# Two scans and an attention: products of the inverses further apart, chain operations ahead on VectorE, weighted values in runs of four

## The chip, the core and the metric

The kernel runs on one core of a Trainium2 chip. The metric is the time of one execution on the device in microseconds (us): the median of several runs of the kernel, and beside it one profiled execution, from which the trace is. TensorE is called PE, its weight loads PEld, VectorE DVE, ScalarE ACT, GpSimd POOL; SP issues the DMAs.

## The reference, cut to what matters

Two blocks follow each other on 2048 tokens of width 1024, all in fp32. The first holds two scans over 256 context tokens and the 2048, in both directions, with 4 heads of width 128 each. The gated delta rule (called gdn below) solves a triangular system in every chunk and then carries a state from chunk to chunk; the gated linear attention (gla) carries one too:

```
A  = strict lower part of (k beta) k^T * decay               # per chunk and head
w, u = (A + I)^-1 [k beta exp(G), v beta]                    # the inverse
v_new = u - w S ;  o = (q exp(G)) S + attn v_new             # the chain over the chunks
S  = S exp(g_last) + k_decayed^T v_new
```

The second block's part of interest is a causal attention of 8 heads, queries and keys of width 96, values of width 64:

```
sc = q k^T / sqrt(96), masked where key > query
o  = softmax(sc) v
out_a = o * silu(z_a)
```

## The kernel before, in words

Matrices that are worth it are split into a high and a low part in the type fp32r, and a product is three matmuls (mm3, lines 188 to 190). The program is written through a layer that schedules: each engine but PE in certain stages gets its order from a planned run of the whole program, in which an instruction with a higher priority goes first among those that are ready. Under manual_schedule PE takes its instructions in the order in which the code emits them. On the chip every engine then works strictly in that order.

**The scans** (lines 885 to 1280, 1055 to 2153 us) are emitted by weave: a planner with a clock of its own. Three streams run: gdn_inverse, gdn_scan and gla_scan. Each is a generator that emits some products and yields (cost, lateness, condition); it may go on when cost and LATE (900 ns) times the lateness have passed on the planner's clock. Between them the planner emits a filler, the projections of rest(): triples of 512 columns (tile d), which are also interleaved where the streams' work is ahead of a share of 0.91. The kernel's chunks are of 128 tokens, 18 for each head and direction.

gdn_inverse makes the inverses of two chunks at a time, 72 times. From the inverses of the 32-wide diagonal blocks (X, Pm = its transpose, E = the part above them) it takes a Neumann series: the product lv1 gives Yt (copied by ACT), then R = X - Yt^T R (direction 0, line 964) or R = 1 - ... (direction 1, lines 975 and 981), each R a tensor_sub on DVE that reads the product lv and is the input of the next. It may be two chunks ahead of gdn_scan. gdn_scan has per chunk the products pa (then r on DVE, line 1022), pv (vn on ACT), pS (the new state S on DVE, line 1037) and po. gla_scan works per block of 256 tokens; its factors (function factors: x, l2, the running sum E, I, F, kc, qs, qh, qc, qk) are made a block ahead on DVE, ACT and POOL, and its products are px, pt, go.

**The attention** (3216 to 3800 us) goes through 8 heads h and 4 groups g of 512 queries. One unit is one block of 128 keys (kb): scores makes the three products into st, ACT takes the exponential into pT, and POOL or DVE adds it up into acc. weigh multiplies pT with the values, in fp32, into one half of po's partitions: even and odd blocks go to different halves of 64 columns of PE, so two neighbours can run side by side. Maxima, queries and keys of later groups (tiles sx, ms) are emitted ahead of the scores, spread evenly over time. weigh is emitted for two blocks at a time, PVL = 4 units after the second. gather comes GL = 2 units later: it adds the halves of po into o2, transposes acc, sums it, takes the reciprocal l4 and spreads it over 64 columns into li; finish, FL = 3 units later for a pair of heads, turns li by a product with the identity and scales o2 with it. po has one buffer, pT six.

Of the kernel before, what the change touches and what calls it, by code (L numbers as in the profile page):

```python
# [21 lines left out]
P = 128  # L22
# [23 lines left out]
SXB = 3  # L46
STB = 2
POB = 1
PTB = 6
QB = 5  # L50
PVL = 4
GL = 2
LIP = 0
AD = 3
VB = 2
DPB = 3
# [6 lines left out]
SHARE = 0.91  # L63
BEG = 37000.0
VBF = 2
PRB = 2
GLEAD = 0
WPRI = 1000
# [24 lines left out]
def block_kernel(ctx: ExitStack, tc: tile.TileContext, A, out):  # L93
# [791 lines left out]
    with ExitStack() as gctx:  # L885
        BW = 256
        nch = BW // P
        with tc.tile_pool(name="c1", bufs=2, side="right") as c1, tc.tile_pool(name="c1s", bufs=1, space=PSUM) as c1s, \
# [25 lines left out]
            def gdn_inverse():  # L914


                B4 = [P, 2, 4, 32]

                def load(t):
                    d, h, i, n = step_at(t)  # L920
                    gdn_blocks(t)
                    gdn_blocks(t + 2)
                    m = n - n % 2
                    Xc, Pc = (x[:, m % 4:m % 4 + 2, :].unsqueeze(2).to_broadcast(B4) for x in blocks[h, d, n // 4])
                    N = c1.tile([P, 2, P], F32, tag="N", name="N", bufs=1)
# [12 lines left out]
                def times(lv, a, b):  # L938
                    for c in range(2):
                        pe.matmul(out=lv[:, c], lhsT=a[:, c], rhs=b[:, c], start=True, stop=True)  # L940

                def sums(tag="lv2"):
                    return c1s.tile([P, 2, P], F32, tag="lv", name=tag)

                one = ident.unsqueeze(1).to_broadcast([P, 2, P])
                nxt = load(0)
                for t in range(0, STEPS, 2):
                    d, h, i, n = step_at(t)
                    X, Pm, E = nxt
                    yield 0.0, 0.0, lambda: t <= at[0] + AHEAD  # L950


                    Yt = new("Yt", 1)
                    if d == 0:
                        lv = sums("lv1")
                        times(lv, E, Pm)
                        act.copy(out=Yt, in_=lv)
                        yield 427.0, 1.0
                        R = X
                        for j in range(3):  # L960
                            lv = sums()
                            times(lv, Yt, R)
                            R = new("R") if j < 2 else new("I")
                            dve.tensor_sub(R, X, lv)
                            if j < 2:
                                yield 427.0, 1.0
                        I = R
                    else:

                        lv = c1s.tile([P, 4, P], F32, tag="lv", name="lv1")  # L970
                        times(lv[:, 2:4], Pm, E)
                        times(lv[:, 0:2], E, Pm)
                        act.copy(out=Yt, in_=lv[:, 2:4])
                        R = new("R")
                        dve.tensor_sub(R, one, lv[:, 0:2])  # L975
                        yield 853.0, 1.0
                        for j in range(2):
                            lv = sums()
                            times(lv, Yt, R)
                            R = new("R")  # L980
                            dve.tensor_sub(R, one, lv)
                            yield 427.0, 1.0
                        lv = sums("lv3")
                        times(lv, X, R)
                        I = new("I")
                        act.copy(out=I, in_=lv)
                    inv[t], inv[t + 1] = I[:, n % 2], I[:, 1 - n % 2]
                    if t + 2 < STEPS:
                        nxt = load(t + 2)
                    yield 427.0, 1.0  # L990

            def gdn_scan():
                def load(t):
# [18 lines left out]
                for t in range(STEPS):  # L1012
# [6 lines left out]
                    if i:  # L1019
                        pa = c1s.tile([P, P], F32, tag="pa", name="pa")  # L1020
                        pe.matmul(out=pa, lhsT=kT, rhs=S, start=True, stop=True)
                        dve.scalar_tensor_tensor(out=r, in0=pa, scalar=c_r[:, d, h, n:n + 1], in1=r, op0=ALU.mult,
                                                 op1=ALU.add)
                        yield 213.0, 1.0
                    pv = c1s.tile([P, P], F32, tag="pa", name="pv")
                    pe.matmul(out=pv, lhsT=X, rhs=r, start=True, stop=True)
# [3 lines left out]
                    if i < NCH - 1:  # L1030
# [3 lines left out]
                        if i == 0:  # L1034
                            dve.tensor_copy(out=Sn, in_=ps)
                        else:
                            dve.scalar_tensor_tensor(out=Sn, in0=S, scalar=eGt[:, d, h, n:n + 1], in1=ps, op0=ALU.mult,
                                                     op1=ALU.add)
                    if n < NT:
                        po = c1s.tile([P, P], F32, tag="po", name="po")  # L1040
                        pe.matmul(out=po, lhsT=pr[:, 1, :], rhs=S, start=True, stop=False)
# [639 lines left out]
    with ExitStack() as actx:  # L1681
# [116 lines left out]
                              in0=ps[0:4, 0:P].unsqueeze(1).to_broadcast([4, 4, P]),  # L1798
                              in1=dmask.unsqueeze(2).to_broadcast([4, 4, P]), op=ALU.mult)

        LI = (dve, pool)[LIP]
        acc_, po_, pT_, o_ = {}, {}, {}, {}

        def scores(h, g, kb):
# [43 lines left out]
        def gather(h, g):  # L1848
# [2 lines left out]
            m, r0_ = h // 2, (h % 2) * 64  # L1851
            if r0_ == 0:
                o_[m, g] = (tb.tile([P, GQ], F32, tag=f"o2{g}", name="o2", bufs=1),
                            tb.tile([P, 4, P], F32, tag=f"li{g}", name="li", bufs=1))
            o2, li = o_[m, g]
            rs_, ro = slice(r0_, r0_ + 64), slice(64 - r0_, P - r0_)
            c0 = P if g == 0 else 0
# [9 lines left out]
            for j in range(4):  # L1867
                pe.transpose(out=ps[:, j, :], in_=acc[:, j * P:(j + 1) * P], identity=ident)
            l4 = tb.tile([P, 4], F32, tag="l4", name="l4")
            dve.tensor_reduce(out=l4, in_=ps, op=ALU.add, axis=AX.X)  # L1870
            dve.reciprocal(out=l4, in_=l4)
            LI.tensor_tensor(out=li[:, :, rs_], in0=on64.unsqueeze(1).to_broadcast([P, 4, 64]),
                              in1=l4.unsqueeze(2).to_broadcast([P, 4, 64]), op=ALU.mult)

        def finish(m, g):

            o2, li = o_.pop((m, g))
            gs = slice(g * GQ, (g + 1) * GQ)
            ps = psa.tile([P, GQ], F32, tag="ms", name="ms", bufs=MSB)
            for j in range(4):  # L1880
                pe.matmul(out=ps[:, j * P:(j + 1) * P], lhsT=li[:, j], rhs=ident, start=True, stop=True)
            z = tb.tile([P, GQ], F32, tag="z", name="z")
            sp.dma_start(out=z, in_=d_za[m, :, gs])
            dve.tensor_mul(o2, ps, o2)
# [86 lines left out]
        with tc.manual_schedule(engines=PE_ONLY):  # L1971
# [8 lines left out]
            f0 = ctx.enter_context(tc.tile_pool(name="f0", bufs=2))  # L1980
            tb = actx.enter_context(tc.tile_pool(name="tb", bufs=2))
            psb = actx.enter_context(tc.tile_pool(name="psb", bufs=2, space=PSUM))
            on64 = tb.tile([P, 64], F32, name="on64", tag="on64", bufs=1)
            pool.memset(on64, 1.0)
            for i in range(4):
                value(0, i)
            now, wait, late = 0.0, [], [2, 3, 4, 5, 6]
            for u, (n, h, g, kb) in enumerate(units):
# [10 lines left out]
                scores(h, g, kb)  # L1999
                if h == 0 and g < NG4 - 1 and kb < 4:  # L2000
                    value(0, 4 * g + 4 + kb)
                if kb % 2:
                    wait += [(u + PVL, weigh, (h, g, k)) for k in (kb - 1, kb)]
                    if h == 3 and g == NG4 - 1:
                        wait += [(u + PVL, value, (1, k)) for k in (kb - 1, kb)]
                if kb == 4 * g + 3:
                    wait.append((u + PVL + GL, gather, (h, g)))
                    if h % 2:
# [59 lines left out]
```

## Time and profile before

| | us |
|---|---|
| median of three runs | 3994.24 (3989.38 to 3999.57) |
| profiled execution | 3978.06 |
| its span | 3976.3 |
| PE busy | 3577.2 (90%) |
| DVE busy | 2481.2 (62%) |
| ACT busy | 1373.1 (35%) |
| POOL busy | 1395.6 (35%) |

The span is the time from the first to the last instruction. Busy times are sums over the whole span, which holds stages of different kinds: projections and preparations up to 1055 us, the scans, the merge to about 2670, the second block's projections to 3216, the attention, and the output projection from 3800 on. Matmuls are pipelined: one of 512 columns is shown with some 0.40 us, while the next begins 0.23 us after it; so the distance of two starts tells what an instruction takes away from others, and idle time of PE is counted only from the modelled end. A row of waits names who waited, for whom, the sum in us, how often, and the longest. A product of two fp32 operands has two records, one in fp32r has one.

### The profile page before, as it was taken

To read this page: it belongs to the slowest core of one execution; us is meant where nothing else is said; L and a number is where in the kernel's file an instruction comes from. 1 tells how busy PE (TensorE), PEld (TensorE's weight loads), DVE (VectorE), ACT (ScalarE), POOL (GpSimd) and SP (SyncE) were. 2 spreads that over 40 slices of the span, in tenths; PEclk is the share of its full clock that TensorE was granted. 3 is DMA by queue.
4 is the path that set the end of the run, shared out by engine and by line. 5 is a ranking of instruction groups with operands and counts; after the bars stand their busy time and mean duration, and the time that the engine had idled before them with its cause. 6 is when DMAs were issued, how large, how long until landed. Compare 5 with 4: busy or idle time off the path is not lost.

```text
span 3976.3 us, 57274 instructions
## 1 busy us (share of the span) xinstructions
PE 3577.2 (90%) x18998; PEld 2868.6 (72%) x18998; DVE 2481.2 (62%) x6394; ACT 1373.1 (35%) x3379; POOL 1395.6 (35%) x1666
## 2 busy tenths in 40 slices
PE   4799998888899999988889787878999999999999
PEld 0578877776788887877777677777888765565577
DVE  3645657887776776666665755546405377777766
ACT  0444542221254444444443322212212244444400
POOL 2310124440355555555552311110122246666610
PEclk7899999999999999999999898988999999999999
DMA  5322347763344444544545433324333510001254
GB/s 155 112 61 76 89 139 244 231 183 67 104 135 127 133 130 132 149 136 140 159 142 145 139 103 98 100 88 125 116 103 112 181 47 26 26 18 44 68 170 148
DMA packets 528220, 467.25 MB, mean 118 GB/s; under 512 B 91705, under 2 KB 446371, under 8 KB 527732
## 3 DMA queue, kind: packets, MB, share of 16 engines
q1 hardware_dynamic: 527700, 463.54, 39.3%
q8 instruction: 151, 2.47, 0.3%
q14 instruction: 145, 1.19, 0.1%
q0 software_dynamic: 224, 0.05, 0.0%
HBM read 302.08 MB, written 161.37 MB: 117 GB/s over the span
## 4 chain that ended last, share of the span: by engine, by line
PE 38%; DMA 9%; DVE 8%; issue 4%; ACT 2%; POOL 1%; SPq 0%; DVEq 0%; ACTq 0%; POOLq 0%
PE d L188 4%; PE d L189 4%; PE d L190 4%; PE po L1845 3%; PE acc L188 2%; PE acc L189 2%; PE acc L190 2%; DMA d_h<-xt 2%; PE sx L1782 2%; DMA mg<-d_gate 2%; PE st L1812 2%; PE lv L940 2%; PE st L1813 1%; PE st L1814 1%; DMA o<-d_ob 1%
## 5 line engine op out<-in xcount | busy, mean ns | idle before, releaser
L188 PE MATMUL d<-uBh,whi 128*128 128x512 f32 x832 | 364.2, 438 | 18.3 <-ACT gy L835 13.1
L188 PE MATMUL d<-uAh,whi 128*128 128x512 f32 x832 | 357.9, 430 | 11.6 <-DVE gy L848 6.0
L189 PE MATMUL d<-uAl,whi 128*128 128x512 f32 x832 | 333.9, 401 | 5.8 <-DVE uAl L464 5.8
L189 PE MATMUL d<-uBl,whi 128*128 128x512 f32 x832 | 334.9, 403 | 0.0
L235 POOL TENSOR_TENSOR wlo<-wraw,whi 128x512 fp32r<-128x512 f32 x128 | 168.4, 1316 | 467.9 <-ACT whi L234 442.4
L190 PE MATMUL d<-uAh,wlo 128*128 128x512 f32 x832 | 332.3, 399 | 0.0
L190 PE MATMUL d<-uBh,wlo 128*128 128x512 f32 x832 | 332.3, 399 | 0.0
L1818 ACT ACTIVATE pT<-st 128x512 f32<-128x512 f32 (+1 forms) x320 | 170.0, 532 | 232.2 <-PE st L1814 139.7
L1836 POOL TENSOR_TENSOR acc<-acc,pT 128x512 f32<-128x512 f32 (+1 forms) x168 | 185.9, 1107 | 120.7 <-ACT pT L1818 110.9
L1787 DVE TENSOR_REDUCE mx<-sx 128x1 f32<-128x512 f32 (+3 forms) x288 | 169.4, 616 | 47.5 <-PE sx L1782 29.0
L1388 POOL TENSOR_TENSOR ml<-mg,mh 128x256 fp32r<-128x256 f32 x64 | 57.4, 896 | 395.5 <-ACT mh L1387 305.5
L188 PEld LDWEIGHTS d<-uBh,whi 128*128 128x128 f32 x832 | 161.0, 194 | 43.7 <-ACT gy L835 14.0
L188 PEld LDWEIGHTS d<-uAh,whi 128*128 128x128 f32 x832 | 160.6, 193 | 35.9 <-ACT pre L769 5.1
L190 PEld LDWEIGHTS d<-uBh,wlo 128*128 128x128 f32 x832 | 159.3, 192 | 35.4
L190 PEld LDWEIGHTS d<-uAh,wlo 128*128 128x128 f32 x832 | 159.4, 192 | 33.8
L189 PEld LDWEIGHTS d<-uAl,whi 128*128 128x128 f32 x832 | 160.4, 193 | 26.8 <-DVE uAl L464 6.4
L189 PEld LDWEIGHTS d<-uBl,whi 128*128 128x128 f32 x832 | 161.3, 194 | 20.1 <-DVE uBl L464 0.4
L940 PE MATMUL lv<-R,Yt 128*128 128x128 f32 x576 | 100.2, 298 | 82.1 <-DVE R L975 48.7
L631 DVE SCALAR_TENSOR_TENSOR y<-st,VT,y 128x512 f32<-128x512 f32 (+1 forms) x224 | 165.0, 769 | 4.6
L188 PE MATMUL pp<-yh,w_a_out_h 128*128 128x256 f32 x256 | 84.4, 330 | 91.1 <-DVE mg L1384 89.9
L1845 PE MATMUL po<-pT,v 128*64 128x512 f32 (+3 forms) x640 | 161.0, 562 | 3.3 <-DVE o L1859 3.3
L940 PEld LDWEIGHTS lv<-R,Yt 128*128 128x128 f32 x576 | 81.3, 197 | 110.5 <-DVE R L975 58.2
(593 smaller groups left out, 10620.3 us busy)
## 6 DMA issues: line engine op xcount, KB each, us to landing
wraw<-in_w_in_dram SPq DMA_DIRECT2D x126, 256.0 KB
k<-d_k SPq DMA_DIRECT2D x144, 192.0 KB
d_p<-pre SPq DMA_DIRECT2D x64, 384.0 KB
d_gate<-gy SPq DMA_DIRECT2D x96, 256.0 KB
rows<-d_rows SPq DMA_DIRECT2D x36, 512.0 KB
pr<-d_p SPq DMA_DIRECT2D x128, 128.0 KB
mg<-d_gate SPq DMA_DIRECT2D x64, 256.0 KB
wm<-in_w_mod_dram SPq DMA_DIRECT2D x24, 512.0 KB
```

The source lines that it names most:

```text
L188: pe.matmul(out=out, lhsT=lh, rhs=rh, start=start, stop=False)
L189: pe.matmul(out=out, lhsT=lh, rhs=rl, start=False, stop=False)
L190: pe.matmul(out=out, lhsT=ll, rhs=rh, start=False, stop=stop)
L235: pool.tensor_tensor(out=lo[:, ks, :n], in0=raw[:, :, :n], in1=hi[:, ks, :n].bitcast(F32), op=ALU.subtract)
L631: dve.scalar_tensor_tensor(out=y[:, :w], in0=st[:, o + j:o + j + w], scalar=tap, in1=y[:, :w], op0=ALU.mult, op1=ALU.add)
L940: pe.matmul(out=lv[:, c], lhsT=a[:, c], rhs=b[:, c], start=True, stop=True)
L1782: pe.matmul(out=ps[:, :w], lhsT=qh[0:96, j * P:(j + 1) * P], rhs=kTh[h % 2][0:96, b * 512:b * 512 + w], start=True, stop=not last)
L1787: dve.tensor_reduce(out=m4[:, j:j + 1] if one else mx[:, j, b:b + 1], in_=ps[:, :w], op=ALU.max, axis=AX.X)
L1812: pe.matmul(out=ps[:, c0:], lhsT=kt_h[0:100, ks], rhs=qh[0:100, c0:], start=True, stop=False)
L1818: act.activation(out=pT[:, c0:], in_=ps[:, c0:], func=AF.Exp, scale=SCALE)
L1836: (dve if on_dve else pool).tensor_tensor(out=acc[:, c0:], in0=src[:, c0:], in1=pT[:, c0:], op=ALU.add)
L1845: pe.matmul(out=po_[h, g][r:r + 64, c0:], lhsT=val[kb][:, vs], rhs=pT_.pop((h, g, kb))[:, c0:], start=kb < 2, stop=kb >= 4 * g + 2, skip_g ...
```

## The change

Five edits, in two stages.

1. SLACK = 1.7: gdn_inverse yields this lateness instead of 1.0 after each of its products.
2. The tensor_sub of R in both directions, r and S of gdn_scan are emitted with high priority (PRI = 1000).
3. weigh is emitted for four key blocks at a time, PVL = 3 units after the fourth; pT has 8 buffers. The values of the second four heads, which replace those of the first, follow in fours as well.
4. gather writes the reciprocal straight into li, now two columns a row, one for each head of a pair; the product with ones is gone.
5. finish spreads both columns over 64 each with one copy (lw) on DVE, ahead of its products. The tile of ones and its memset are gone.

```
+SLACK = 1.7
-PTB = 6
+PTB = 8
-PVL = 4
+PVL = 3
...
                         times(lv, E, Pm)
                         act.copy(out=Yt, in_=lv)
-                        yield 427.0, 1.0
+                        yield 427.0, SLACK
                         R = X
                         for j in range(3):
                             lv = sums()
                             times(lv, Yt, R)
                             R = new("R") if j < 2 else new("I")
-                            dve.tensor_sub(R, X, lv)
+                            with tc.high_priority(PRI):
+                                dve.tensor_sub(R, X, lv)
                             if j < 2:
-                                yield 427.0, 1.0
+                                yield 427.0, SLACK
...
-                        dve.tensor_sub(R, one, lv[:, 0:2])
-                        yield 853.0, 1.0
+                        with tc.high_priority(PRI):
+                            dve.tensor_sub(R, one, lv[:, 0:2])
+                        yield 853.0, SLACK
...
-                        dve.scalar_tensor_tensor(out=r, in0=pa, scalar=c_r[:, d, h, n:n + 1], in1=r, op0=ALU.mult,
-                                                 op1=ALU.add)
+                        with tc.high_priority(PRI):
+                            dve.scalar_tensor_tensor(out=r, in0=pa, scalar=c_r[:, d, h, n:n + 1], in1=r, op0=ALU.mult,
+                                                     op1=ALU.add)
...
-            dve.reciprocal(out=l4, in_=l4)
-            LI.tensor_tensor(out=li[:, :, rs_], in0=on64.unsqueeze(1).to_broadcast([P, 4, 64]),
-                              in1=l4.unsqueeze(2).to_broadcast([P, 4, 64]), op=ALU.mult)
+            dve.reciprocal(out=li[:, :, h % 2], in_=l4)
...
+            lw = tb.tile([P, 4, 2, 64], F32, tag="lw", name="lw", bufs=1)
+            dve.tensor_copy(out=lw, in_=li.unsqueeze(3).to_broadcast([P, 4, 2, 64]))
...
-                if kb % 2:
-                    wait += [(u + PVL, weigh, (h, g, k)) for k in (kb - 1, kb)]
+                if kb % 4 == 3:
+                    wait += [(u + PVL, weigh, (h, g, k)) for k in range(kb - 3, kb + 1)]
```

How the order of PE changes in the scans, at the place that the trace has at 1711 us: what stands between the first product of an inverse (lv1) and the next (lv2) in direction 1. Before:

```order
L940 MATMUL lv1_17427<-Pm_17315,E_17316 128x128 x2
L188 MATMUL d_17378<-uBh_758,whi_16993 128x512
L189 MATMUL d_17378<-uBl_759,whi_16993 128x512
L190 MATMUL d_17378<-uBh_758,wlo_16994 128x512
L1231 MATMUL go_17438<-S_17324,qc_17163 128x128
L1232 MATMUL go_17438<-v_17057,at_15581 128x128
L940 MATMUL lv2_17445<-R_17433,Yt_17426 128x128 x2
```

The same on PE of the changed kernel, from the two products go on; ahead of them stand the same lv1 and the same triple (lines from 959 on have moved down by up to five):

```order
L1236 MATMUL go_17438<-S_17322,qc_17174 128x128
L1237 MATMUL go_17438<-v_17057,at_15593 128x128
L1030 MATMUL pv_17451<-r_17384,I_17345 128x128
L188 MATMUL d_17378<-uBh_758,whi_16993 128x512
L189 MATMUL d_17378<-uBl_759,whi_16993 128x512
L190 MATMUL d_17378<-uBh_758,wlo_16994 128x512
L940 MATMUL lv2_17458<-R_17433,Yt_17426 128x128 x2
```

A second triple and pv have come between; they stood behind lv2 before.

On DVE at the second inverse of direction 1, where R (line 975, then 977) is the subtraction and F, qk, x, l2 and qc are factors of gla_scan. Before:

```order
L1125 TENSOR_TENSOR F_15774<-I_15775,E_15731 128x2x4
L1126 TENSOR_TENSOR F_15774<-I_15775 128x2x4
L1131 COPY F_15774<-I_15775 128x2
L1127 TENSOR_TENSOR F_15774<-F_15774 128x2x2
L1129 TENSOR_TENSOR F_15774<-F_15774 128x2x2
L1165 TENSOR_TENSOR qk_15827<-qs_15825,F_15774 128x2x64
L1166 TENSOR_TENSOR qk_15827<-ke_15815,F_15774 128x2x64
L1105 SCALAR_TENSOR_TENSOR x_15969<-x_15969,l1_15978 128x256
L1163 TENSOR_TENSOR qc_15826<-qs_15825,F_15774 128x256
L1106 TENSOR_TENSOR l2_15979<-l2_15979,l1_15978 128x256
L975 TENSOR_TENSOR R_15549<-ident_117,lv1_15543 128x256
```

On DVE of the changed kernel the same subtraction and what follows it:

```order
L1167 TENSOR_TENSOR qs_15825<-qs_15825,q_15821 128x256
L1166 TENSOR_TENSOR qh_15823<-qh_15823,q_15821 128x256
L977 TENSOR_TENSOR R_15546<-ident_117,lv1_15540 128x256
L1230 SCALAR_TENSOR_TENSOR S_15552<-S_15453,F_15227,px_15511 128x128
L1130 TENSOR_TENSOR F_15788<-I_15789,E_15754 128x2x4
L1131 TENSOR_TENSOR F_15788<-I_15789 128x2x4
L1136 COPY F_15788<-I_15789 128x2
L1132 TENSOR_TENSOR F_15788<-F_15788 128x2x2
L1134 TENSOR_TENSOR F_15788<-F_15788 128x2x2
L1170 TENSOR_TENSOR qk_15827<-qs_15825,F_15788 128x2x64
```

R has moved ahead of the chain of F and all that follows from it.

On PE in the attention, around one pair of blocks before (st are scores, po weighted values, ms queries):

```order
L1812 MATMUL st_33754<-qh_33071,kTh0_31605 128x512
L1813 MATMUL st_33754<-ql_33072,kTh0_31605 128x512
L1814 MATMUL st_33754<-qh_33071,kTl0_31607 128x512
L1845 MATMUL po_33728<-pT_33659,v_31971 64x512
L1845 MATMUL po_33728<-pT_33691,v_31977 64x512
L188 MATMUL ms_33765<-ch_31468,wuh_33401 128x512
```

And on PE of the changed kernel, around the run that holds the same two blocks (sx are maxima):

```order
L1818 MATMUL st_33732<-qh_33067,kTl0_31607 128x512
L1849 MATMUL po_33739<-pT_33631,v_31957 64x512
L1849 MATMUL po_33739<-pT_33643,v_31963 64x512
L1849 MATMUL po_33739<-pT_33654,v_31969 64x512
L1849 MATMUL po_33739<-pT_33690,v_31975 64x512
L1787 MATMUL sx_33744<-kTh1_31606,qh_33427 128x384
```

Two runs of two have become one of four, and four blocks of scores now follow each other without weighted values between them.

## Rows read from the trace of the kernel before

**Rows 1.** busy us by engine, PE clock, DMA; scans, then attention

```profile
1055.00:2153.00 1098.00, 985.20 (x6288) 859.94 (x6287) 746.23 (x2169) 505.09 (x1609) 576.87 (x845) 0.98 0.48 137
3216.00:3800.00 584.00, 568.26 (x2750) 342.12 (x2750) 418.32 (x741) 267.57 (x510) 356.02 (x311) 0.98 0.11 36
```

**Rows 2.** who waited for whom in the scans: us in total, times, longest

```profile
PE lv L940 <- DVE R L975: 48.7, 30, 6.3
PE lv L940 <- DVE R L964: 21.5, 27, 2.4
PE lv L940 <- DVE R L981: 11.3, 11, 3.6
PE pS L1032 <- ACT vn L1028: 10.8, 15, 2.1
```

**Rows 3.** groups by line in the scans: busy us, mean ns, idle before

```profile
L940 PE MATMUL lv<-R,Yt 128*128 128x128 f32 x576 | 100.2, 298 | 82.1 <-DVE R L975 48.7 <-DVE R L964 21.5 <-DVE R L981 10.9
L1193 PE MATMUL px<-ident,kc 128*128 128x128 f32 x144 | 40.0, 278 | 0.6 <-DVE S L1225 0.6
L981 DVE TENSOR_TENSOR R<-ident,lv 128x256 f32<-128x256 f32 x72 | 29.9, 416 | 14.6 <-PE lv L940 14.2
```

**Rows 4.** PE in order of time at 1711 us: start, us, line

```profile
1711.47 0.40 PE L190 MATMUL d<-uBh,wlo 128*128 128x512 f32 x1
1711.70 0.38 PE L1231 MATMUL go<-S,qc 128*128 128x128 f32 x2
1711.92 0.39 PE L1232 MATMUL go<-v,at 128*128 128x128 f32 x2
1716.48 0.84 PE L940 MATMUL lv<-R,Yt 128*128 128x128 f32 x4 [4.17 <-DVE R L975]
```

**Rows 5.** instructions of DVE in order of time, the same place

```profile
1712.80 1.03 DVE L1165 TENSOR_TENSOR qk<-qs,F 128x128 f32<-128x128 f32 x1 [2.13 <-ACT F L1132]
1715.68 0.41 DVE L1163 TENSOR_TENSOR qc<-qs,F 128x256 f32<-128x256 f32 x1
1716.02 0.41 DVE L975 TENSOR_TENSOR R<-ident,lv 128x256 f32<-128x256 f32 x1
```

**Rows 6.** instructions of PE in order of time, a pair of weighted values

```profile
3562.62 0.40 PE L1814 MATMUL st<-qh,kTl 96*128 96x512 f32 x1
3562.95 1.08 PE L1845 MATMUL po<-pT,v 128*64 128x512 f32 x4
3563.96 0.27 PE L1796 MATMUL ms<-ident,m 128*4 128x128 f32 x1
```

**Rows 7.** the same, pairs whose later blocks are narrower

```profile
3507.22 1.07 PE L1845 MATMUL po<-pT,v 128*64 128x512 f32 x4
3508.22 0.39 PE L188 MATMUL ms<-wkvh,kvh 128*128 128x256 f32 x1
3510.58 0.65 PE L1845 MATMUL po<-pT,v 128*64 128x256 f32 x4
3511.15 0.38 PE L188 MATMUL ms<-wkvh,kvh 128*128 128x256 f32 x1
```

**Rows 8.** the same, three pairs that stand together at the end

```profile
3787.11 2.36 PE L1845 MATMUL po<-pT,v 128*64 128x512 f32 x12
3789.40 0.51 PE L188 MATMUL acc<-wz,a 128*128 128x512 f32 x1
```

**Rows 9.** weight loads of the weighted values: ns min/median/max, starts

```profile
L1845 PEld LDWEIGHTS po<-pT,v x640: 132/136/232, 3226.2 to 3788.9; 128*64 128x64 f32 x160
```

**Rows 10.** who waited for whom in the attention: us in total, times, longest

```profile
PE po L1845 <- DVE o L1859: 3.3, 3, 2.1
PE sx L1782 <- DVE mx L1787: 4.3, 3, 2.5
PEld st L1812 <- ACT pT L1818: 29.1, 39, 0.8
```

**Rows 11.** a group by line of DVE in the attention

```profile
L1872 DVE TENSOR_TENSOR li<-on,l 128x256 f32<-128x256 f32 x32 | 25.7, 804 | 0.1
```

More of the change, by code (lines that the diff above doesn't have):

```diff
@@ L48 @@
 POB = 1
-PTB = 6
+PTB = 8
 QB = 5
-PVL = 4
+PVL = 3
 GL = 2
-LIP = 0
 AD = 3
@@ L980, in gdn_inverse @@
                             R = new("R")
-                            dve.tensor_sub(R, one, lv)
-                            yield 427.0, 1.0
+                            with tc.high_priority(PRI):
+                                dve.tensor_sub(R, one, lv)
+                            yield 427.0, SLACK
                         lv = sums("lv3")
@@ L989, in gdn_inverse @@
                         nxt = load(t + 2)
-                    yield 427.0, 1.0
+                    yield 427.0, SLACK
             def gdn_scan():
@@ L1021, in gdn_scan @@
                         pe.matmul(out=pa, lhsT=kT, rhs=S, start=True, stop=True)
-                        dve.scalar_tensor_tensor(out=r, in0=pa, scalar=c_r[:, d, h, n:n + 1], in1=r, op0=ALU.mult,
-                                                 op1=ALU.add)
+                        with tc.high_priority(PRI):
+                            dve.scalar_tensor_tensor(out=r, in0=pa, scalar=c_r[:, d, h, n:n + 1], in1=r, op0=ALU.mult,
+                                                     op1=ALU.add)
                         yield 213.0, 1.0
@@ L1036, in gdn_scan @@
                         else:
-                            dve.scalar_tensor_tensor(out=Sn, in0=S, scalar=eGt[:, d, h, n:n + 1], in1=ps, op0=ALU.mult,
-                                                     op1=ALU.add)
+                            with tc.high_priority(PRI):
+                                dve.scalar_tensor_tensor(out=Sn, in0=S, scalar=eGt[:, d, h, n:n + 1], in1=ps,
+                                                         op0=ALU.mult, op1=ALU.add)
                     if n < NT:
@@ L1799, in shift @@
                               in1=dmask.unsqueeze(2).to_broadcast([4, 4, P]), op=ALU.mult)
-        LI = (dve, pool)[LIP]
         acc_, po_, pT_, o_ = {}, {}, {}, {}
@@ L1853, in gather @@
                 o_[m, g] = (tb.tile([P, GQ], F32, tag=f"o2{g}", name="o2", bufs=1),
-                            tb.tile([P, 4, P], F32, tag=f"li{g}", name="li", bufs=1))
+                            tb.tile([P, 4, 2], F32, tag=f"li{g}", name="li", bufs=1))
             o2, li = o_[m, g]
@@ L1879, in finish @@
             ps = psa.tile([P, GQ], F32, tag="ms", name="ms", bufs=MSB)
+            lw = tb.tile([P, 4, 2, 64], F32, tag="lw", name="lw", bufs=1)
+            dve.tensor_copy(out=lw, in_=li.unsqueeze(3).to_broadcast([P, 4, 2, 64]))
             for j in range(4):
-                pe.matmul(out=ps[:, j * P:(j + 1) * P], lhsT=li[:, j], rhs=ident, start=True, stop=True)
+                pe.matmul(out=ps[:, j * P:(j + 1) * P], lhsT=lw[:, j].rearrange("p a b -> p (a b)"), rhs=ident, start=True, stop=True)
             z = tb.tile([P, GQ], F32, tag="z", name="z")
@@ L1982, in block_kernel @@
             psb = actx.enter_context(tc.tile_pool(name="psb", bufs=2, space=PSUM))
-            on64 = tb.tile([P, 64], F32, name="on64", tag="on64", bufs=1)
-            pool.memset(on64, 1.0)
             for i in range(4):
@@ L2001, in block_kernel @@
                     value(0, 4 * g + 4 + kb)
-                if kb % 2:
-                    wait += [(u + PVL, weigh, (h, g, k)) for k in (kb - 1, kb)]
+                if kb % 4 == 3:
+                    wait += [(u + PVL, weigh, (h, g, k)) for k in range(kb - 3, kb + 1)]
                     if h == 3 and g == NG4 - 1:
-                        wait += [(u + PVL, value, (1, k)) for k in (kb - 1, kb)]
+                        wait += [(u + PVL, value, (1, k)) for k in range(kb - 3, kb + 1)]
                 if kb == 4 * g + 3:
```

## The prediction

> **What bounds the kernel now.** I read the busy times of TensorE (PE) first, by stretches, because 90% over the whole span is a mean over stages with different limits. The order of the instructions changes in two stretches alone: the scans (1055 to 2153 us) and the attention (3216 to 3800 us). In the scans PE is busy 985.2 of 1098 us, so 113 us are open; in the attention 568.3 of 584 us, so 16 us are open; VectorE (DVE) is busy 68% and 72% there [rows 1]. The clock was 0.98 in both, the upper level, and the change takes no pause of PE that would tell otherwise. Next I read who waited for whom in the scans. PE stood 48.7 + 21.5 + 11.3 = 81.5 us, in 68 waits, before a product of the inverses (tile lv) until VectorE had written R from the product before it [rows 2]; the group's own row says the same, 82.1 us [rows 3]. That is seven tenths of what PE leaves open there. The third view is the place of one such wait in order of time. The product stands behind five others, a fill of three at 0.23 us each and two small ones at 0.22, and then PE is idle 4.17 us [rows 4]. VectorE in that time first waits 2.13 us for ScalarE, then works through the factors of the other scan, and takes R up only at 1716.02, for 0.41 us [rows 5]. The wait is for VectorE's queue, not for the subtraction. In the attention PE hardly waits; what can be had there is in how its work is packed.
>
> **Scans: the spacing.** The planner emits the next product of an inverse not 0.9 but 1.53 us of planned time after the last (LATE x SLACK). Total work and the rest of PE's order stay: from the end of the inverses on, the same instructions stand at the same rows of the order. At the place above, what stands between two products grows from one fill and two small products, 0.69 + 0.44 = 1.13 us, to two fills and three small ones, 0.69 x 2 + 0.66 = 2.04 us. I counted so through all 216 products that wait for a result of the one before, with 0.23 us for a product of 512 columns, 0.22 for a small one and 0.11 for a transpose [rows 4]: on average 1.42 us before, 2.25 after, at the least 1.02 and 1.82. By kind, the cover grows 1.0 us for L964 and 0.98 for L981 (1.32 to 2.32 for the kind that both feed), and 0.64 for L975 (1.38 to 2.01). A wait shrinks by that, and not below zero. L964: a mean wait of 21.5/27 = 0.80 us is nearly all covered; with a longest of 2.4 I leave 4. L981: 11.3/11 = 1.03; I leave 4. L975: 48.7/30 = 1.62; were all of them longer than 0.64, 30 x 0.64 = 19 would go; I leave 29. Gone: 81.5 - 37 = 44 us. Idle time in the trace begins only at the modelled end of the product before, so short stalls that the pipeline hides are not in the 81.5; that and the next edit bring the term to 50. Bounds: from the side of no gain 0, if what is late is VectorE and comes later by as much; on the other side all 82 + 11 (vn, [rows 2]) = 93.
>
> What the later products make late: the last product of an inverse to the first use of its result had 9.8 (direction 0) and 11.6 us (direction 1) of PE work between them, and now 6.1 and 7.6, by the same count; a result needs about 1 us behind its product. From an inverse's end to the next one's first product there were 5.9 and 6.5 us, now 3.3 and 4.1; the inputs Pm and E stand ready long before, only X waits for the inverse's end, and X is first read one product later. I count both at nothing; if that cover were gone, it would cost 72 inverses x 1 us.
>
> **Scans: the priority.** R, r and S stand ahead of factor work on VectorE wherever both are ready in the planned time. This adds no instruction. At the second inverse of direction 1, R moves ahead of the whole chain of F; at 1716 us it stays behind qk, x and qc as before, so it doesn't cure the longest waits (that is why I leave 29 us to L975). I give it 3 us of the 50 above; bounds -10 to +15, as factors come later by R's 0.42 us [rows 3] each.
>
> **Attention: four key blocks at a time.** A pair of blocks is two products into the two halves of PE's columns, side by side. The pair begins 0.33 us after the product before it, where 0.23 is the rule, and the next product follows 1.01 us after its start [rows 6]: 1.11 us a pair, in time taken from other products. Narrower pairs take 1.00 and 0.57 us [rows 7]. At the kernel's end three pairs of these widths already stand together: 2.29 us [rows 8], against 1.01 + 1.00 + 0.57 and two more beginnings at 0.10, 2.78. So each merge saves 0.49/2 = 0.245 us. The order has 158 runs of them before and 80 after, 78 merges x 0.245 = 19 us. The rule that speaks against it: the Trainium skill, "TensorE: Matmul & The Clock Gate", Part 3, What overlaps and what doesn't, says that a weight load overlaps with a running matmul only where the row groups differ, and all these weights take the same 128 rows. By that rule a junction would show at least one load of 136 ns [rows 9], 78 x 0.136 = 11 us less, and the attention would bring 8 instead of 19; the run of three at the end holds two junctions, and its 2.29 us don't show the loads. Hence 19 stands.
>
> With it go two waits. The first run of a group of queries stood at the same step as the gather that empties po; now it comes two steps behind: 3.3 us [rows 10] go. And in a row of four score blocks without weighted values VectorE's maxima and ScalarE's exponentials get less time: they cost PE 4.3 us for sx, and 29.1 us on the weight loads, which mostly run beside matmuls [rows 10]. I add 4 us; bounds 0 and 20, that is 0.25 us for each of 80 runs, where the merge would be eaten up. pT has 8 buffers and 7 are alive when a run begins.
>
> The broadcast product li (32 x 0.80 = 25.7 us of VectorE [rows 11]) becomes 16 copies of twice its width. In the order the copy stands right behind the reciprocal, three blocks ahead of PE's use, and VectorE has 28% open, so I count it at 0; its cover gone, it would cost 16 x 1 us at most.
>
> **Sum.** 50 + 19 + 3 - 4 = 68 us. The profiled execution took 3978.06 us, 3976.3 of it in the span, so 3910; the median of the runs shown, 3994.24, is 0.41% above it, and on that scale the sum is 3926 us.
>
> **The rivals.** Scan gains given back: VectorE is the engine that is late at [rows 5], and PE's waits turn into later factors. For it: VectorE's 746 us would have to fit in some 1050, 71%, and it works in bursts. Against it: 350 us of VectorE are idle in the scans. Only the attention's 18 would stay: 3960, on the median's scale 3976. More than forecast: the waits for R go altogether, and those for vn with them, 93 + 18 = 111 us: 3883 after scaling; for it the least cover of 1.82 us, against it the 4.17 us. Slower: R, S and r, placed ahead, wait at the head of VectorE's queue for their products, as R does already for 14.2 us [rows 3], and the factors behind them come too late for the transposes of kc (L1193), which wait 0.6 us now [rows 3]. There are 72 blocks of factors; from 1 us a block it eats the whole gain, at 1.5 us it costs 108 against 68: 4034 us. Against it: VectorE's idle time, and factors are made a block ahead.
>
> **How the numbers follow.** Forecast 0.62; gains of the scans given back 0.17; more than forecast 0.13; slower 0.05; a small rest, 0.03, where both parts come to nothing. What a measurement of this kernel can tell from no change is about 0.3%, 12 us. Faster: 0.62 + 0.13 + 12 parts of the 0.17 (18 us is just over the bound) = 0.87; same 0.08; slower 0.05. The range: 3880, all waits gone, to 3986, the attention alone with half of its gain eaten by its own new waits.
>
> **What would show it.** Right: PE's waits on R near 35 us, the scans' stretch near 1050 us, PE still busy 985 in it; 80 runs of x8 at about 1.9 us or less, the attention near 566 us. Wrong: a new large wait before px or pv, R's wait for lv on VectorE far above 25 us in total, or PE idle before sx and st by more than 10 us.

## The result and the profile after

| | median of the runs, us | profiled execution, us |
|---|---|---|
| before | 3996.01 (3989.38 to 3999.57, 4 runs) | 3978.06 |
| after | 3945.17 (3941.75 to 3950.95, 4 runs) | 3950.95 |

The ratio is 0.9876 (95% interval 0.9858 to 0.9894): 49.5 us faster (42 to 57), where 68 were forecast; 3945 lies in the range, 19 us above the predicted time. The profiled execution of before was 18 us under its median and that of after 6 above, so these two traces differ by 27 us only. Sizes are therefore taken from medians and from further traces of both orders; the two traces tell where the time stands.

Busy times by stretch after, answering to [rows 1] (PE, PEld, DVE, ACT, POOL, then PE's granted clock, DMA share, GB/s):

```profile
1054.00:2130.00 1076.00, 985.61 (x6291) 865.37 (x6290) 733.56 (x2168) 503.46 (x1609) 574.93 (x845) 0.97 0.49 139
3196.00:3775.00 579.00, 553.88 (x2762) 360.92 (x2761) 417.17 (x727) 265.67 (x509) 360.96 (x311) 0.97 0.11 37
```

For the same work the scans took 22 us less with PE busy for the same 985 us; the attention took 5 less with PE busy for 14 less. So the scans lost idle time, and the attention lost work but gained idle time. Who waited for whom in the scans after, answering to [rows 2] (total us, times, longest us):

```profile
PE lv L940 <- DVE R L977: 30.1, 21, 4.2
PE pv L1030 <- DVE r L1026: 25.3, 28, 3.6
PE pa L1024 <- DVE S L1042: 5.3, 5, 1.4
PE px L1198 <- DVE S L1228: 4.7, 4, 1.7
PE lv L940 <- DVE R L965: 2.1, 4, 1.0
```

And the group rows of the products that waited, answering to [rows 3] (busy us, mean ns, idle us before); the last one is pv in the kernel before:

```profile
L940 PE MATMUL lv<-R,Yt 128*128 128x128 f32 x576 | 94.1, 287 | 33.6 <-DVE R L977 30.1 <-DVE R L965 2.1 <-DVE R L984 1.0
L1030 PE MATMUL pv<-r,I 128*128 128x128 f32 x288 | 61.4, 296 | 26.3 <-DVE r L1026 25.3 <-DVE I L965 0.5
L1026 PE MATMUL pv<-r,I 128*128 128x128 f32 x288 | 58.7, 286 | 5.5 <-DVE r L1022 4.9 <-DVE I L964 0.5
```

The inverses' wait fell from 82.1 to 33.6 us: 48.5 went, where 44 were forecast. The wait of pv is new in its size: 5.5 us before and 26.3 now, for r of the chain. S is waited for 10.0 us (before 0.6). Some 30 of the 48.5 us that left R are back on r and S.

The longest waits that are left are of the kind at [rows 4, 5]. PE after, in order of time at 1701 us (start, duration, line; in brackets the idle time before; some rows):

```profile
1701.78 0.39 PE L190 MATMUL d<-uBh,wlo 128*128 128x512 f32 x1
1706.39 1.22 PE L940 MATMUL lv<-R,Yt 128*128 128x128 f32 x4 [4.22 <-DVE R L977]
1708.48 0.63 PE L189 MATMUL d<-uBl,whi 128*128 128x512 f32 x1
1708.91 0.63 PE L190 MATMUL d<-uBh,wlo 128*128 128x512 f32 x1
```

DVE in the same time:

```profile
1702.62 1.03 DVE L1170 TENSOR_TENSOR qk<-qs,F 128x128 f32<-128x128 f32 x1 [2.33 <-ACT F L1137]
1703.57 0.81 DVE L1171 TENSOR_TENSOR qk<-ke,F 128x128 f32<-128x128 f32 x1
1704.31 0.94 DVE L1110 SCALAR_TENSOR_TENSOR x<-x,l 128x256 f32<-128x256 f32 x1
1705.17 0.41 DVE L1111 TENSOR_TENSOR l<-l,l 128x256 f32<-128x256 f32 x1
1705.50 0.50 DVE L1168 TENSOR_TENSOR qc<-qs,F 128x256 f32<-128x256 f32 x1
1705.93 0.41 DVE L977 TENSOR_TENSOR R<-ident,lv 128x256 f32<-128x256 f32 x1
```

As before, R stands behind a block of factors that itself waits for ScalarE. There is a second thing to see: behind the pause PE's products are longer, 0.63 us where 0.39 was the rule. The granted clock of these stretches fell at the same time (columns as above):

```profile
1700.00:1705.00 5.00, 2.17 (x13) 1.55 (x12) 2.67 (x4) 2.39 (x7) 2.76 (x4) 0.99 0.42 116
1705.00:1710.00 5.00, 3.61 (x13) 3.32 (x14) 3.41 (x12) 0.27 (x1) 1.84 (x3) 0.50 0.57 160
```

PE stood still from 1702.17 to 1706.39. The clock was at the upper level (2.4 GHz, 0.99) until 1705, within the pause, and at the lower (1.2 GHz, 0.50) in the 5 us in which PE went on.

In the attention, a run of four blocks where a pair stood, answering to [rows 6, 7]:

```profile
3508.00 0.40 PE L1818 MATMUL st<-qh,kTl 96*128 96x512 f32 x1
3508.33 1.94 PE L1849 MATMUL po<-pT,v 128*64 128x512 f32 x8
3510.20 0.50 PE L1816 MATMUL st<-qh,kTh 100*128 100x512 f32 x1
```

The run takes 1.87 us from its start to the next product's. There are 80 runs of 8 records: 46 take 1.87 us, 30 with narrower blocks 1.43 to 1.44, and 4 take 2.0 to 2.9. PE's waits there, answering to [rows 10]:

```profile
PE sx L1787 <- DVE mx L1792: 6.8, 7, 2.7
PE ms L1885 <- DVE m L1794: 3.1, 1, 3.1
PE ms L1872 <- DVE acc L1869: 2.9, 1, 2.9
PE ms L1801 <- DVE m L1794: 2.5, 2, 1.6
PE ms L188 <- DVE l L1874: 2.2, 2, 1.4
```

The wait of po for the gather (3.3) is gone. The waits of products into ms have grown: from the first product into st to the last weighted value they sum to 15.7 us, before to 6.4, and the largest row of them before was this one:

```profile
PE ms L1796 <- DVE m L1789: 2.9, 2, 2.2
```

### The profile page after: what moved, and what is told of

Its sections match the earlier page's. It is cut to its first block, busy times and chain, and to the rows that moved or that the text cites. A ratio compares the mean times of both kernels' runs of the same rounds, so it can differ in the third digit from the quotient of the medians.

```text
span 3949.2 us, 57199 instructions
## 1 busy us (share of the span) xinstructions
PE 3557.5 (90%) x18998; PEld 2886.1 (73%) x18998; DVE 2467.2 (62%) x6378; ACT 1370.0 (35%) x3379; POOL 1400.1 (35%) x1665
## 4 chain that ended last, share of the span: by engine, by line
PE 32%; DMA 9%; DVE 5%; issue 4%; ACT 2%; POOL 1%; SPq 0%; DVEq 0%; ACTq 0%; POOLq 0%
PE d L188 3%; PE po L1849 3%; PE d L189 3%; PE d L190 3%; PE acc L188 2%; PE acc L189 2%; PE acc L190 2%; DMA d_h<-xt 2%; DMA mg<-d_gate 2%; PE sx L1787 2%; PE st L1816 2%; PE st L1817 1%; PE st L1818 1%; DMA o<-d_ob 1%; DMA raw<-in_w_in_dram 1%
## 5 line engine op out<-in xcount | busy, mean ns | idle before, releaser
L234 ACT CAST whi<-wraw 128x512 fp32r<-128x512 f32 x128 | 78.2, 611 | 216.6 <-DMA wraw<-in_w_in_dram 170.0
L1849 PE MATMUL po<-pT,v 128*64 128x512 f32 (+3 forms) x640 | 143.0, 547 | 0.0
L818 DVE TENSOR_TENSOR Mt<-M 128x1 f32<-128x1 f32 (+40 forms) x155 | 135.8, 876 | 4.0
```

The source lines that it names most:

```text
L818: dve.tensor_tensor(out=t, in0=M[:w, i:i + 1, i + 1:32].to_broadcast([w, L, L]), in1=M[:w, i + 1:32, i + 1:32].rearrange("p j c -> p c j") ...
L1849: pe.matmul(out=po_[h, g][r:r + 64, c0:], lhsT=val[kb][:, vs], rhs=pT_.pop((h, g, kb))[:, c0:], start=kb < 2, stop=kb >= 4 * g + 2, skip_g ...
```

## The experiments

Ratios are to runs of the kernel before on the same chip. "Scans" is the time from the first product of an inverse to the first of the merge (pp), "attention" from the first product into st to the last weighted value, both of one trace each; the scans so measured end some 33 us behind the stretches of [rows 1].

| run | median, us | ratio, 95% interval | scans | attention |
|---|---|---|---|---|
| before (first trace) | | 1 | 1130.8 | 571.7 |
| after (first trace) | 3945.17 | 0.9876 (0.9858 to 0.9894) | 1108.9 | 565.1 |
| attention edits alone | 3974.21 | 0.9978 (0.9968 to 0.9988) | 1131.6 | 561.9 |
| spacing alone | 3956.27 | 0.9923 (0.9910 to 0.9937) | 1104.4 | 572.2 |
| priorities alone | 3983.74 | 0.9998 (0.9985 to 1.0011) | 1131.9 | 575.5 |
| after, again | 3938.20 | 0.9882 (0.9868 to 0.9895) | 1101.0 | 561.8 |
| + r later | 3906.69 | 0.9815 (0.9793 to 0.9837) | 1063.6 | 561.4 |
| + one running sum | 3931.38 | 0.9880 (0.9858 to 0.9903) | 1092.9 | 556.8 |
| + spacing 2.4 | 3922.92 | 0.9860 (0.9835 to 0.9884) | 1088.1 | 568.6 |
| + lw earlier | 3943.62 | 0.9908 (0.9889 to 0.9926) | 1102.2 | 563.3 |
| r later, spacing 1.0 | 3959.22 | 0.9941 (0.9924 to 0.9958) | 1114.4 | 565.9 |
| + gather later | 3935.59 | 0.9873 (0.9857 to 0.9888) | 1104.1 | 551.6 |
| all later, running sum | 3906.76 | 0.9802 (0.9787 to 0.9818) | 1058.2 | 568.4 |
| + r and gather later | 3889.33 | 0.9769 (0.9748 to 0.9789) | 1061.9 | 553.1 |

**The parts apart.** Three kernels hold one part each; the fourth is the changed kernel again.

```
attention alone:   SLACK = 1.0, no high_priority
spacing alone:     weigh, li, PTB, PVL of before; no high_priority
priorities alone:  the same, SLACK = 1.0, high_priority(1000) at R, r, S
```

> The attention edits and the new reciprocal product alone; the spacing of the inverses is back at 1.0 and no priorities are set. Theory A (the forecast's split): the attention brings 18 us, so about 3978 if before stands at 3996. Theory B (the two traces' split: first score product to last weighted value shrank by 6.6 us only): about 3989, a gain of 7, because new waits of sx and ms give back what the merges save.

> The spacing of 1.7 alone, without the priorities and with the attention of before. Theory A: 47 to 50 us less than before, about 3946. Theory B (the scans' stretch of the two traces: 1094.4 to 1071.5 us): about 23 less, 3973, because the waits for R turn into waits for r.

> The priorities alone: spacing 1.0, attention of before. Forecast's theory: about 3 us faster than before, and R ahead of the chain of F at the second inverse of direction 1. Rival: the instructions stand in the same order as before on every engine, so the time is that of before within 0.1%, and this run is a second measurement of before. The rival 'slower' of the prediction would put it above before.

> The changed kernel as it is, a second measurement with a second trace. Expected 3945, 50 us under before. If the two parts add up, a1 and a2 together gain what this one gains; what is missing from the sum is their interaction.

Measured: 9 us (5 to 13) for the attention, 31 (25 to 36) for the spacing, nothing for the priorities, 47 (42 to 53) for the whole. Both sizes lie between the two theories, nearer to B. The parts sum to 40, which the intervals don't tell from 47. The priorities leave every engine's instructions in the order of before, row for row. The same holds at the wider spacing: up to the end of the scans, spacing alone has every engine's instructions in the order of the changed kernel, which has the priorities too. The run with the priorities alone is so a second trace of before, and against the second one of after the scans come out as in the medians, 1131.9 to 1101.0; the attention falls by 14 us, from 575.5 to 561.8, where the medians gave 9.

**What r waits for.** Two theories: the spacing from pa to pv is too small for r now (Cover), or VectorE's queue is too full (Queue).

```
 gdn_scan, behind r:    -yield 213.0, 1.0        +yield 213.0, SLACK          (r later)
 factors:  -dve.tensor_copy(out=I[:, :, 0], in_=tm[:, :, 0])                  (running sum)
           -for b in range(1, 4): dve.tensor_add(I[:, :, b], I[:, :, b - 1], tm[:, :, b])
           +dve.tensor_tensor_scan(out=If, data0=m4, data1=tau, ...)   # reversed in direction 1
 SLACK:    -1.7   +2.4                                                        (spacing 2.4)
```

> The changed kernel, with the product pv emitted 1.53 instead of 0.90 us of planned time after pa, so that VectorE has more time for r. In the changed kernel pv waits 25 to 29 us for r. Theory Cover (r's wait is a lack of PE work between pa and pv, as R's was): 28 waits shorten by some 0.6 us, 12 to 17 us less, ratio to before 0.985. Theory Queue (VectorE's queue is the limit and a longer spacing only moves the wait on, to S, the next R or the transposes of kc): within 5 us of the changed kernel, ratio 0.988.

> The changed kernel, with the four small sums that begin a block of factors (a copy and three adds, 114 us of VectorE in the scans) made by one running sum. The result is the same. Theory Queue: R and r stand behind these in VectorE's queue; the waits for them (29 + 29 us) fall by a third or more, 15 to 25 us less than the changed kernel, ratio 0.983. Theory Cover: the burst is not what is late; R's and r's waits stay above 50 us together and the time is within 5 us of the changed kernel.

> The changed kernel with a spacing of 2.4 instead of 1.7. Theory Cover: the 29 us that are left to the wait for R fall by another 0.6 us each, below 15, and the time by 10 us or more, ratio 0.985. Theory Queue: R's wait falls and r's and S's grow by as much, as from 1.0 to 1.7; the time is within 5 us of the changed kernel. A third way: the inverses now end too late for the products that use them, a new wait for I on PE, and the time is above the changed kernel's.

r's spacing alone brought another 22 to 37 us: 3906.69 is 73.0 under its before, where the changed kernel is 46 to 51 under its own, and a kernel with the same order of instructions (lw earlier, below) 36 under it on this chip. That is more than Cover forecast. The two waits in the scans of after, again, and then the waits with r later:

```profile
PE lv L941 <- DVE R L978: 29.2, 21, 4.4
PE pv L1031 <- DVE r L1027: 28.7, 29, 4.0
```

```profile
PE lv L941 <- DVE R L978: 14.9, 13, 1.7
PE pa L1025 <- DVE S L1043: 9.3, 9, 2.4
PE pS L1037 <- ACT vn L1033: 9.0, 21, 1.2
PE pv L1031 <- DVE r L1027: 8.8, 12, 1.9
```

r's wait fell from 28.7 (after, again) to 8.8, and R's from 29.2 to 14.9 though no product was put between two products of an inverse. The scans as a whole, with the same 6403 to 6405 records of products; before, first trace:

```profile
1055.00:2186.00 1131.00, 1012.30 (x6404) 881.35 (x6402) 762.31 (x2213) 517.63 (x1626) 579.45 (x847) 0.98 0.48 138
1540.00:2060.00 520.00, 454.10 (x2875) 395.60 (x2874) 350.27 (x1017) 233.46 (x708) 282.99 (x401) 0.98 0.51 144
```

After, again:

```profile
1053.00:2154.00 1101.00, 1007.58 (x6403) 882.55 (x6401) 751.52 (x2212) 515.42 (x1626) 576.29 (x847) 0.98 0.49 141
1540.00:2060.00 520.00, 464.03 (x2918) 405.81 (x2918) 344.50 (x1038) 232.46 (x708) 282.50 (x404) 0.97 0.51 148
```

With r later:

```profile
1051.00:2115.00 1064.00, 992.96 (x6405) 871.93 (x6402) 766.50 (x2209) 521.73 (x1627) 579.03 (x847) 0.99 0.51 147
1540.00:2060.00 520.00, 483.62 (x3142) 423.44 (x3141) 379.15 (x1097) 246.76 (x751) 295.97 (x424) 1.00 0.54 156
```

From before to after idle time fell from 118.7 to 93.4 us, and busy time by 5, which is no more than two traces of one order differ by (1013.3 us in the first trace of after). From after to r later idle time fell to 71.0, and busy time by 14.6 more: in direction 1 (the second row of each) the longest wait for R was 4.4 us and is 1.7, and the granted clock is 1.00 instead of 0.97. Of the 37 us by which the scans are shorter three fifths are pauses and two fifths are busy time. The clock fits the second part: in the scans of after, again, PE was busy for 39.5 us while the granted clock stood at its lower level, with r later for 13.6. With products of 512 columns 0.43 us apart there and 0.23 at the upper level, that is an estimate of 12 of the 14.6 us.

The running sum took VectorE's busy time in the scans from 751.5 to 710.6 us, and the waits stayed:

```profile
PE lv L941 <- DVE R L978: 30.4, 20, 5.1
PE pv L1031 <- DVE r L1027: 24.7, 22, 4.8
```

So less work on VectorE didn't shorten them, and Queue in that form falls. (The scans' stretch, 1092.9, is still 8 us under the shortest trace of the changed kernel's order; where those come from is open.) It doesn't show that no work there matters: at 1702 us it is qk, x, l and qc that stand ahead of R, none of which the edit touched. Why R itself comes earlier with r later is seen, not settled: by a count over the traces, the first R of direction 1 starts over 1.5 us behind its product in 26 places with r later, and in these VectorE was at I and F for 48 us in all; in after, again, there are 27 such places, and it was at I for 8 us and at x, l, kc and qk for 37. The two scans meet at other points. No run held that point alone.

The spacing of 2.4 ended the wait for R (no row is left) and took r's to 14.2; yet its interval overlaps with that of after, again (beside lw earlier on the same chip it is 21 us faster). Its stretches show where the gain went. With 2.4, the body of the scans and their end:

```profile
1080.00:2060.00 980.00, 932.73 (x6046) 824.00 (x6047) 624.49 (x2052) 484.81 (x1542) 539.37 (x814) 1.00 0.51 148
2064.00:2149.00 85.00, 43.55 (x283) 38.80 (x281) 45.30 (x113) 30.32 (x69) 23.39 (x26) 0.75 0.50 144
```

The body is idle for 47 us in 980 (1.7: 78.6 in 987). But the fillers between the products are used up at 2101 us, and PE then stands 23.2 + 15.2 us before the merge's first transposes, which wait for loads; in the changed kernel fillers run until 2151 and PE is busy for 77.3 of the last 84 us. Much of the gain was given back at the end of the stage.

**r's spacing without the inverses'.**

```
 SLACK = 1.0;  gdn_scan, behind r:  yield 213.0, 1.7
```

> The changed kernel with the spacing of the inverses back at 1.0 and only r's own spacing (pa to pv) at 1.7; the attention is the changed one. In the kernel before r was waited for 4.9 us only. If the gain of 25 us that r's spacing brought on top of the changed kernel is r's wait alone, little is to be had here: the time of the attention edits alone (ratio 0.998) less at most 5 us, 0.997. If r's spacing works in another way (fewer long pauses of PE and so a higher granted clock, also behind the waits for R), it brings 15 us or more here too, 0.994 or less.

Measured: 0.9941, some 15 us less than the attention edits alone (0.9978): the size of the second theory, far over the 5 of the first. The two ratios come from different chips, but the scans say the same, 1131.6 to 1114.4. Its waits in the scans:

```profile
PE lv L942 <- DVE R L979: 37.3, 26, 5.0
PE lv L942 <- DVE R L967: 19.6, 21, 2.2
PE lv L942 <- DVE R L986: 6.2, 9, 1.4
PE pv L1032 <- DVE r L1028: 2.0, 4, 1.1
```

R is waited for 63.1 us instead of 81.5, although r itself had cost only 4.9. So r's spacing also helps R: a product pv moved by some 0.6 us lets other products fill the places where R was waited for (between a product of lv and the next that reads its R, 9.7 records of products stand on average, 8.3 before). The second theory's reason isn't borne out: the clock in the scans is 0.98 as before, and the gain is idle time.

**The copy lw and the gather.**

```
 lw earlier:     the copy from finish() to behind the reciprocal of the second head in gather()
 gather later:   -GL = 2   +GL = 3
```

> The changed kernel, with the copy lw issued right behind the reciprocal that it reads, three key blocks ahead of its products, instead of right ahead of them. The one wait of 3.1 us on PE for lw goes and with it the small ones for it, 3 to 4 us in the attention (first score product to last weighted value 558 us instead of 561 to 565); the whole is too near for the medians. If the copy is not what is late there, nothing changes.

> The changed kernel, with the gather of a group of queries one score block later, at the distance from the group's end that it had before. Theory: the new pauses of PE in the attention before products of ms (16.0 us, before 6.4) come from the gather and the finish standing one block earlier, so that acc, l4 and lw are late; they fall back to about 7 to 9, and the stretch from the first score product to the last weighted value to 553 us. Rival: they come from the rows without weighted values, where VectorE and ScalarE have less time; then they stay at 16 and the stretch at 561. For the whole time both say within 10 us of the changed kernel.

lw earlier moved no instruction: every engine has the order of the changed kernel, since the planned run had already put the copy close behind the reciprocal. So this run doesn't test the copy's place; the pause of 3.1 us before finish's products and 16 us of pauses before ms stayed. It is a third set of runs of the changed kernel's order, and its ratio, 0.9908, beside 0.9876 and 0.9882, says by how much ratios from different chips can differ: the gain was 49.5, 47 and 37 us. What stands ahead of the pause is the rest of VectorE's queue. After, DVE there; the pause ends at 3600.89:

```profile
3596.77 2.58 DVE L1840 TENSOR_TENSOR acc<-pT 128x512 f32<-128x512 f32 x1
3599.27 1.48 DVE L1883 COPY lw<-li 128x512 f32<-128x512 f32 x1
3600.67 0.14 DVE L1794 TENSOR_REDUCE m<-mx 128x1 f32<-128x2 f32 x1
```

With the gather a block later, the theory's numbers came: pauses before ms 5.7 us, the stretch 551.6. Before st they rose from 2.4 to 5.7, so a third of the gain is lost there. The largest rows of both, then DVE at the same place:

```profile
PE st L1817 <- ACT pT L1823: 4.7, 3, 3.5
PE ms L1873 <- DVE acc L1870: 1.9, 1, 1.9
```

```profile
3597.18 0.12 DVE L1795 TENSOR_REDUCE m<-mx 128x1 f32<-128x2 f32 x1
3597.29 0.71 DVE L1884 COPY lw<-li 128x512 f32<-128x512 f32 x1
```

The attention of after, again, and with the gather later:

```profile
3187.00:3749.00 562.00, 537.05 (x2696) 346.17 (x2695) 411.43 (x716) 264.94 (x508) 361.24 (x311) 0.98 0.12 38
```

```profile
3197.00:3748.00 551.00, 532.90 (x2693) 343.67 (x2692) 409.97 (x716) 265.62 (x508) 358.71 (x311) 0.98 0.12 38
```

Idle time falls from 25.0 to 18.1 us and busy time by 4. The idle time is the safer of the two: from the first product into st to the last weighted value it is 24.2 to 26.3 us in all nine traces with the changed attention and GL = 2, and 17.7 and 16.6 in the two with GL = 3, while the stretch of the nine runs from 556.8 to 568.6, with PE busy for 10 to 33 us of it at the lower level of the clock. In the median the gain is within the intervals (0.9873 against 0.9882).

**All later, and the version that the runs point to.**

```
 all later:           SLACK 2.0, behind r 1.7, behind vn 1.5, running sum
 r and gather later:  SLACK 1.7, behind r SLACK, GL = 3
```

> The changed kernel with spacings of 2.0 for the inverses, 1.7 for r and 1.5 for vn (pv to pS), and the running sum in the factors. Theory Cover: the waits for R (15 us with r's spacing alone) and vn (9) halve again, no long pause of PE is left and the low level of the clock goes with them; 5 to 15 us below r's spacing alone, ratio 0.979 or less. Theory of a floor: with r's spacing the scans already stand near the sum of their products, and the rest of the waits moves on to S and kcs; ratio 0.981 to 0.983.

> The changed kernel with the two edits that the runs point to: r's spacing at 1.7 and the gather one score block later. If they add up (25 us and 3 to 10 us), the ratio to before is 0.979 to 0.981, and both stretches show it: scans near 1025 us, attention near 552. If the gather's gain is lost again behind the attention, the ratio stays at 0.9815.

All later is 0.9802, between the two theories and inside the interval of r later. As the theory of a floor said, waits moved to kcs (15.1 us, with r later 8.3) and to S before pa (12.8, 9.3). But its scans don't stand at the sum of their products: idle time fell to 63.7 us, yet pauses of 2.4 to 3.5 us were left in direction 1 and PE was busy for 39.1 us at the lower level of the clock, where r later had 13.6. The last kernel's ratio is the lowest: 0.9769, 91 us (84 to 100) under before, below the forecast of 0.979 to 0.981. Its trace holds both gains, attention 553.1 as forecast and scans 1061.9; the 1025 forecast for the scans was missed, they stand where r later alone had them.

## Why the prediction was right, and where it was not

**The inverses' waits: right.** Of 82.1 us (81.5 in the rows of waits) 44 were to go and 48.5 went; L964 and L981 nearly vanish (2.1 and 1.0 us are left), L975 keeps 30.1 where 29 was left. The count of products between two products of an inverse gave that number.

**The scans' term: too large, by some 20 us.** 50 were forecast, the spacing alone brought 31 (25 to 36). The step that failed is "What the later products make late": I looked at the users of the inverse (I, X) and found cover, and left out r and S, which share VectorE and the moment with R. They took back 20 and 9 us. The rival of scan gains given back named the mechanism, VectorE being late elsewhere, and part of it happened; but it expected later factors, and r and S of the chain were late. Its reason was half wrong: a spacing for r, with no work less on VectorE, freed more than was missing. A sign of being wrong that the prediction named, a large new wait before pv, did come: 26.3 us.

**The clock.** I wrote that the change takes no pause of PE that would tell otherwise. The pause of 4.22 us above is followed by the lower level, and with r later, where the longest waits are shorter, the same products take 15 us less. The changed kernel kept pauses as long as 4.2 us, so it got none of that: direction 1 had 0.98 before and 0.96 to 0.97 after.

**The priority: wrong.** 3 us were credited to it, and the slower rival was built on it. It moves no instruction, neither alone nor with the spacing; R's place ahead of the chain of F, which I put down to it, comes from the spacing.

**The attention: price right, new waits too small.** 19 us for 78 merges at 0.245: PE's busy time from the first product into st to the last weighted value fell from 556.4 to 537.3 (after, again), 19.1 us; a run of 8 records takes 1.87 us. The rule on weight loads that I weighed against it (the Trainium skill, "TensorE: Matmul & The Clock Gate", Part 3, What overlaps and what doesn't) would have left 8; the trace disagrees with it here: 80 runs hold 80 junctions of two pairs, and 19 us went all the same. In the run at 3508.33 the two loads at 3509.24 (136 ns each) lie inside the products that start there and run to 3509.83, over the same 128 rows, and the next pair starts 0.43 us after. The 3 us for po came (3.3). The term of new waits was 4 us and measured some 12: pauses before ms rose from 6.4 to 16.0 (after, again), before sx and st by 3 together. I looked for them at sx and st, in the rows without weighted values; most of them came from PVL = 3, which puts gather and finish a block earlier than before, against acc and l on VectorE. The copy counted at nothing is 0.86 us each, 12.9 for the 15 that fall into the stretch, and delays m and with it PE at one place only. Its cover was read too large: in the trace of after, again, 0 to 3 blocks of scores stand between the copy and PE's use, about one as a rule, and not three.

**The sum.** 50 + 19 + 3 - 4 = 68 became about 30 + 19 + 3 - 12 = 40 by the parts and 37 to 50 by the whole, in three sets of runs. The time lies in the range because the range was 106 us wide: the two main mechanisms were right, and two terms, the scans' and the new waits', were mis-sized by 20 and 8 us. The stretches of [rows 1] show it, 1076 us where 1050 was forecast and 579 where 566 was.

## What to carry to other kernels

When two chains share an engine, giving one of them more time moves the wait to the other: price every result that the shared engine writes, not only those whose distance is edited, and space them together. Watch too what the spacing uses up: fillers that are spent earlier leave the end of the stage bare. And a tiling that saves PE time shifts everything that hangs on its steps; put those steps back where they stood.

## What the runs showed of the hardware that I had not expected

- The granted clock fell from the upper to the lower level within a stage that is busy for over 90%: it was 0.50 in the 5 us in which a pause of 4.22 us ended, and products of 512 columns then stood 0.43 us apart instead of 0.23. With r later, where the longest wait for R is 1.7 us, the same 6400 records of products were busy for 993 us instead of 1008, and for 13.6 instead of 39.5 of it at the lower level.
- The price of a tiny sum on VectorE goes with what GpSimd does beside it: I<-I,E of 128x2 took 417 ns on average in the scans of after, again, no less than a subtraction of 128x256 (R, 416), but that mean hides two kinds. All 60 that ran beside no GpSimd instruction took 145 to 166 ns; the 156 that ran beside one took 147 to 1273, so every longer one is among them. No run took the GpSimd work away, so the cause is not shown. One running sum over eight columns took 326 or 405 ns on average, by direction, and replaced four such instructions.
